# Sharing eleven semaphores among the transfers, and storing tile 58 in pieces of 48, 50 and 30 rows

## The chip, the cores and the metric

One core of one Trainium2 chip. The metric is device time in microseconds (us) of one execution. The span of a profile is about 1.8 us shorter than that time. All runs told here were in the fast state, and all gave the right result.

## The reference

```python
# x (16, 512, 1024), weight (1024, 768), bias (768), residual (16, 512, 768), all float32
def reference(x, weight, bias, residual):
    return (np.matmul(x, weight) + bias + residual).astype(np.float32)
```

That is 8192 rows: 64 tiles of 128 rows, with K = 1024 and N = 768. 61.9 MB are read and 25.2 MB written.

## The kernel before

The kernel records its operations in a list and then emits them with only the waits that they need. SyncE issues every transfer, in the order of a fixed list. An entry `('s', 3, 10, 11, 104)` stores tile 3 x 16 + 10 = 58, cut at row 104, so in two transfers of 104 and 24 rows. Each row of a tile is 3 KB.

```python
ORDER = [
 # ... loads of x, weight, bias and residual, and the stores of tiles 0 to 47
 ('s', 3, 0, 10), ('s', 3, 10, 11, 104), ('s', 3, 11, 13),          # tiles 48-57; 58; 59-60
 ('s', 3, 13, 14), ('s', 3, 14, 15), ('c', 3, 15, 0), ('c', 3, 15, 1)]   # 61; 62; 63 in two column parts

# in Program.emit, one semaphore for each transfer:
        for n, (eng, emit, _, dma) in enumerate(ops):
            e = self.engines[eng]
            for d in waits[n]:
                e.wait_ge(*mark[d])
            ins = emit(e)
            if dma:
                sem = self.tc.alloc_semaphore(f"landed_{n}")
                mark[n] = (sem, 16)
                ins.then_inc(sem, 16)
            # ... compute instructions count up the semaphore of their engine

# in pump(), a store with its cuts:
                edges = [0, *cut, P]
                for p0, p1 in zip(edges, edges[1:]):
                    dma(out_d[S, p0:p1, j0:j1, n0:n0 + nl],
                        R[p0:p1, t0 % RR:t0 % RR + j1 - j0, n0:n0 + nl], ...)   # cut
                    stores.append(len(prog.ops) - 1)

# at the end: all stores must have landed
        for sem, value in landed[:-OUTSIDE]:                 # OUTSIDE = 4
            nc.sync.wait_ge(sem, value)
    # ... and in a second critical section the last four, in reverse order
```

Of the kernel before, what the change touches and what calls it, by code (L numbers as in the profile page):

```python
# [31 lines left out]
 ('r', 0, 6, 16), ('x', 0, 14, 16), ('x', 1, 0, 6), ('r', 1, 0, 6), ('x', 1, 6, 16),  # L32
 ('r', 1, 6, 16), ('s', 0, 0, 16), ('x', 2, 0, 6), ('r', 2, 0, 6), ('x', 2, 6, 16),
 ('r', 2, 6, 16), ('s', 1, 0, 16), ('x', 3, 0, 6), ('r', 3, 0, 7), ('x', 3, 6, 16),
 ('r', 3, 7, 16), ('s', 2, 0, 16), ('s', 3, 0, 10), ('s', 3, 10, 11, 104), ('s', 3, 11, 13),
 ('s', 3, 13, 14), ('s', 3, 14, 15), ('c', 3, 15, 0), ('c', 3, 15, 1)]
OUTSIDE = 4
LAST = [(0, 512), (512, 256)]
# [2 lines left out]
class Program:  # L41
# [10 lines left out]
    def add(self, eng, emit, rd=(), wr=(), dma=False):  # L52
        n, ops = len(self.ops), self.ops
        deps = {self.writer[k] for k in (*rd, *wr) if k in self.writer and (eng != "pe" or ops[self.writer[k]][0] != eng)}
        for k in wr:
            deps.update(d for d in self.readers.get(k, ()) if ops[d][0] != eng or ops[d][3])
        for k in rd:
            self.readers.setdefault(k, set()).add(n)
        for k in wr:
            self.writer[k], self.readers[k] = n, set()  # L60
        self.ops.append((eng, emit, deps - {n}, dma))

    def emit(self, ends):

        ops, known = self.ops, {e: {} for e in self.engines}
        lane, count, snap, waits = [], {}, [], []
        for n, (eng, _, deps, dma) in enumerate(ops):
            mine = (n, 0) if dma else (eng, count.setdefault(eng, 0) + 1)
            if not dma:
                count[eng] += 1  # L70
            seen = known[eng]
            need = {}
            for d in deps:
                f, i = lane[d]
                if seen.get(f, -1) < i and i > need.get(f, (-1, 0))[0]:
                    need[f] = (i, d)
            need = {
                f: (i, d) for f, (i, d) in need.items()
                if not any(snap[d2].get(f, -1) >= i for g, (_, d2) in need.items() if g != f)
            }  # L80
            for f, (i, d) in need.items():
                for g, v in (*snap[d].items(), (f, i)):
                    if seen.get(g, -1) < v:
                        seen[g] = v
            waits.append([d for _, d in need.values()])
            lane.append(mine)
            own = dict(seen)
            own[mine[0]] = mine[1]
            snap.append(own)
        told = {d for w in waits for d in w}  # L90
        sems = {e: self.tc.alloc_semaphore(f"done_{e}") for e in self.engines if e != "sp"}
        total, mark = dict.fromkeys(self.engines, 0), {}
        for n, (eng, emit, _, dma) in enumerate(ops):
            e = self.engines[eng]
            for d in waits[n]:
                e.wait_ge(*mark[d])
            ins = emit(e)
            if dma:
                sem = self.tc.alloc_semaphore(f"landed_{n}")
                mark[n] = (sem, 16)  # L100
                ins.then_inc(sem, 16)
            elif n in told:
                total[eng] += 1
                mark[n] = (sems[eng], total[eng])
                ins.then_inc(sems[eng], 1)
        return [mark[n] for n in ends]
# [3 lines left out]
def kernel(  # L110
# [136 lines left out]
    def times(po, lhsT, rhs, first, final, rd, wr):  # L247
        def emit(e):
            return e.add_instruction(mybir.InstMatmult(  # L249
                name=nc.get_next_instruction_name(),  # L250
                ins=[e.lower_ap(rhs), e.lower_ap(lhsT, for_matmul_weights=True)], outs=[e.lower_ap(po)],
                start_tensor_calc=first, stop_tensor_calc=final,
                tile_size=(P, P), tile_position=(0, 0), ldweights=False,
            ))
        op("pe", emit, rd, wr)
# [144 lines left out]
```

## Time and profile before

| | before |
|---|---|
| time, median of 3 runs | 210.88 us (210.81 to 211.23) |
| span of the profile | 209.1 us |
| TensorE busy | 200.4 us, 96% |
| transfer queue, share of 16 engines | 97.7% |
| end of the last matmul | 204.1 us |

Two lines of the profile's page, kernel before: the busy share of the transfer engines in 40 slices of the span, in tenths, and what they moved.

```profile
DMA  6999999999989999999999999999999999998994
GB/s 222 424 429 436 432 414 471 391 449 411 495 377 486 389 410 418 442 447 407 428 450 450 411 423 479 404 423 412 424 482 423 421 415 472 451 432 366 441 360 162
```

Read them with the share of TensorE: two resources are nearly full at once. (The 16 engines that carry transfers are called transfer engines here. The records name no engine. The numbers 0 to 15 are labels: a store with 13 late counts is said to lie on engines 0 to 12, one with 12 on 0 to 11. Within a trace the rows bear such an order out: in the kernel before, twelve engines take ten rows of tile 58, one takes eight and three none. That an engine keeps its label in another execution or another kernel is an assumption.) TensorE ends at 204.1 us and the transfers run on behind it, so each can set the end, and only the last few microseconds tell which. The chain of waits, in order of time, shows the computing part of that end (columns: start, length, what):

```profile
198.89 5.21 PE psum_o L249 x32
204.11 0.02 issue
204.13 0.43 DVE ro L221
```

VectorE's last add is done at 204.56 us. The other 4.6 us of the span are stores landing and the closing barriers.

### The profile page before, as it was taken

The numbers are of one execution on the slowest core, as the hardware profiler recorded it, in microseconds if no ns is written. First come the engines' busy times: TensorE is split into PE (matmuls) and PEld (weight loads), VectorE is DVE, ScalarE is ACT, GpSimd is POOL, SyncE is SP. The second block draws the span as 40 slices with busy tenths as digits, with TensorE's granted clock in tenths as the row PEclk, the third lists the DMA queues.
The fourth block names the chain that finished last, engine by engine and source line by source line (L and its number), as shares of the span: only waits on it lengthen the run. The fifth ranks groups of instructions, "written<-read, shape, count | busy, mean of one in ns | idle before, by whom it ended". The sixth has DMA issues, their size and how long they took to land.

```text
span 209.1 us, 2471 instructions
## 1 busy us (share of the span) xinstructions
PE 200.4 (96%) x1273; PEld 80.9 (39%) x794; DVE 105.3 (50%) x141; ACT 66.1 (32%) x69; POOL 115.1 (55%) x71
## 2 busy tenths in 40 slices
PE   7899999999999999999999999999999999999990
PEld 2333433443443344344434433443443344344440
DVE  1458555445545544654455454645545544554451
ACT  2444513402640372310370093320091055330000
POOL 1100029759999805998039702999108950999000
PEclk9999999999999999999999999999999999999997
DMA  6999999999989999999999999999999999998994
GB/s 222 424 429 436 432 414 471 391 449 411 495 377 486 389 410 418 442 447 407 428 450 450 411 423 479 404 423 412 424 482 423 421 415 472 451 432 366 441 360 162
DMA packets 4924, 87.20 MB, mean 417 GB/s; under 512 B 557, under 2 KB 685, under 8 KB 1841
## 3 DMA queue, kind: packets, MB, share of 16 engines
q1 hardware_dynamic: 4913, 87.05, 97.7%
q8 instruction: 8, 0.13, 0.2%
q14 instruction: 3, 0.02, 0.0%
HBM read 61.88 MB, written 25.17 MB: 416 GB/s over the span
## 4 chain that ended last, share of the span: by engine, by line
PE 91%; DMA 4%; issue 1%; DVE 1%; SPq 0%; ACT 0%
PE psum_o L249 78%; PE pt L242 13%; DMA x_tile<-in_x_dram 4%; SPq L160 0%; DVE xt L218 0%; ACT xb L218 0%; DVE ro L221 0%; SPq L395 0%; SPq L363 0%
## 5 line engine op out<-in xcount | busy, mean ns | idle before, releaser
L249 PE MATMUL psum_o<-w_sb,xt 128*128 128x256 bf16 (+1 forms) x999 | 175.3, 324 | 1.8 <-DVE xt L218 0.5
L221 POOL TENSOR_TENSOR ro<-ro,bias_sb 128x768 f32<-128x768 f32 x50 | 88.8, 1811 | 46.8 <-DMA ro<-in_residual_dram 46.8
L218 ACT CAST xb<-x_tile 128x1024 bf16<-128x1024 f32 (+1 forms) x63 | 61.3, 1023 | 117.1 <-DMA x_tile<-in_x_dram 80.1
L260 PEld LDWEIGHTS <-xt 128*128 128x128 bf16 x520 | 50.9, 98 | 102.9 <-issue 101.0
L218 DVE COPY xt<-pt 128x1024 bf16<-128x1024 bf16 x64 | 44.1, 691 | 83.6 <-PE pt L242 83.6
L221 DVE TENSOR_TENSOR ro<-psum_o,ro 128x768 f32<-128x768 f32 (+2 forms) x51 | 47.6, 934 | 6.3 <-POOL ro L221 4.3
L242 PE MATMUL pt<-ident,xb 128*128 128x128 f32 x256 | 38.3, 273 | 0.5 <-DVE xb L218 0.3
L221 POOL TENSOR_TENSOR ro<-ro 128x768 f32<-128x768 f32 x14 | 24.9, 1813 | 25.0 <-DMA ro<-in_residual_dram 25.0
L242 PEld LDWEIGHTS pt<-ident,xb 128*128 128x128 f32 x256 | 29.7, 140 | 15.5 <-issue 12.3
L221 DVE TENSOR_TENSOR ro<-psum_o,bias_sb 128x768 f32<-128x768 f32 x14 | 13.2, 948 | 0.0
L304 PE MATMUL psum_o<-warm 128*128 128x512 bf16 x18 | 6.4, 514 | 1.4 <-DVE warm_a L224 1.4
L218 DVE CAST xb<-x_tile 128x512 bf16<-128x512 f32 (+1 forms) x4 | 1.9, 492 | 6.1 <-DMA x_tile<-in_x_dram 6.1
L218 ACT CAST w_sb<-ro 128x768 bf16<-128x768 f32 x4 | 3.3, 832 | 3.7 <-DMA ro<-in_weight_dram 3.7
L218 POOL CAST w_sb<-ro 128x768 bf16<-128x768 f32 x1 | 0.8, 824 | 5.9 <-DMA ro<-in_weight_dram 5.9
L304 PEld LDWEIGHTS psum_o<-warm 128*128 128x128 bf16 x18 | 2.2, 126 | 4.6 <-issue 2.9
L218 DVE CAST w_sb<-ro 128x768 bf16<-128x768 f32 x3 | 1.7, 557 | 2.0 <-DMA ro<-in_weight_dram 2.0
L218 ACT ACT_TABLE_LOAD x1 | 1.3, 1283 | 0.9 <-SPq L363 0.9
L321 DVE STREAM_SHUFFLE bias_sb<-bias_row 128x768 f32<-128x768 f32 x1 | 1.0, 1024 | 0.0
L224 DVE MEMSET warm<- 128x256 uint32 x1 | 0.3, 272 | 1.1 <-SPq L363 1.1
L224 DVE MEMSET bias_row<- 128x768 f32 x1 | 0.7, 698 | 0.2 <-issue 0.2
L224 POOL MEMSET ident<- 128x128 f32 x1 | 0.2, 204 | 0.5 <-SPq L363 0.5
L312 POOL TENSOR_SCALAR_AFFINE_SELECT ident<-ident 128x128 f32<-128x128 f32 x1 | 0.3, 293 | 0.2 <-POOL ident L224 0.2
(7 smaller groups left out, 0.7 us busy)
## 6 DMA issues: line engine op xcount, KB each, us to landing
out_dram<-ro SPq DMA_DIRECT2D x3, 6144.0 KB, 34.4
x_tile<-in_x_dram SPq DMA_DIRECT2D x3, 5120.0 KB, 24.5
ro<-in_residual_dram SPq DMA_DIRECT2D x3, 3840.0 KB, 32.1
x_tile<-in_x_dram SPq DMA_DIRECT2D x3, 3072.0 KB, 39.8
ro<-in_residual_dram SPq DMA_DIRECT2D x3, 2304.0 KB, 18.5
x_tile<-in_x_dram SPq DMA_DIRECT2D x4, 1024.0 KB, 10.9
x_tile<-in_x_dram SPq DMA_DIRECT2D x2, 2048.0 KB, 23.4
out_dram<-ro SPq DMA_DIRECT2D x1, 3840.0 KB, 13.1
```

Source lines behind the costliest of these rows:

```text
L218: op(eng, lambda e: (e.copy if eng == "act" else e.tensor_copy)(out=dst, in_=src), rd, wr)
L221: op(eng, lambda e: e.tensor_add(out=dst, in0=a, in1=b), rd, wr)
L224: op(eng, lambda e: e.memset(dst, v), [], [wr])
L242: op("pe", lambda e, q=q: e.transpose(out=pt[:, q, :], in_=words[:, ts(q, P)], identity=ident), [("XB", t % XB_N, 2 * q // n_q), "ident"], ...
L249: return e.add_instruction(mybir.InstMatmult(name=nc.get_next_instruction_name(), ins=[e.lower_ap(rhs), e.lower_ap(lhsT, for_matmul_weight ...
L260: op("pe", lambda g: g.ldweights(lhsT), rd)
L304: op("pe", lambda e: e.matmul(PO[i][:, 0:512], lhsT=warm[:, 0:P], rhs=warm, start=True, stop=True), ["warm"], [("PO", i)])
L312: op("pool", lambda e: e.affine_select(out=ident, in_=ident, compare_op=mybir.AluOpType.not_equal, fill=1.0, base=0, pattern=[[-1, P]], ch ...
L321: op("dve", lambda e: e.stream_shuffle(out=bias_sb, in_=bias_row, mask=[0] * QUAD), ["bias_row"], ["bias"])
```

## The change

The intent has two parts. A semaphore may serve a second transfer once SyncE has seen the first land, so eleven do for all, and fewer have to be cleared at the end. And the pieces of tile 58 are cut so that the transfer engines taken to be late get fewer of its rows.

```diff
- ('r', 3, 7, 16), ('s', 2, 0, 16), ('s', 3, 0, 10), ('s', 3, 10, 11, 104), ('s', 3, 11, 13),
+ ('r', 3, 7, 16), ('s', 2, 0, 16), ('s', 3, 0, 10), ('s', 3, 10, 11, 48, 98), ('s', 3, 11, 13),
@@ in emit
-        lane, count, snap, waits = [], {}, [], []
+        lane, count, snap, waits, slots, slot = [], {}, [], [], [], {}
@@
+            if dma:
+                free = [i for i, used in enumerate(slots) if seen.get(used[-1], -1) >= 0]
+                if not free:
+                    free = [len(slots)]
+                    slots.append([])
+                slot[n] = free[0], len(slots[free[0]]) + 1
+                slots[free[0]].append(n)
@@
+        landings = [self.tc.alloc_semaphore(f"landed_{i}") for i in range(len(slots))]
@@
-                sem = self.tc.alloc_semaphore(f"landed_{n}")
-                mark[n] = (sem, 16)
-                ins.then_inc(sem, 16)
+                i, k = slot[n]
+                mark[n] = (landings[i], 16 * k)
+                ins.then_inc(landings[i], 16)
```

The transfers go from 36 to 37 and the program's semaphores from 46 to 21: 36 and 11 for transfers, the other ten the same.

## The prediction

> **What bounds the kernel now.** I read the chain that ended last first, then the stretches after the last matmul, then the last stores, and at last the single records of stores and transfers in the same trace.
>
> ```profile
> ## 4 chain that ended last, share of the span: by engine, by line
> PE 91%; DMA 4%; issue 1%; DVE 1%; SPq 0%; ACT 0%
> ...
> q1 hardware_dynamic: 4913, 87.05, 97.7%
> q8 instruction: 8, 0.13, 0.2%
> ```
>
> TensorE carries the chain from about 10 us to 204.1 us of the 209.1 us span, and nothing in the change touches it. But the transfer queue is as full: 97.7% of 16 engines' time. So whatever a store leaves behind at the end cannot hide. Next, the stretches at the end (columns: stretch, its length, busy time and count of PE, PEld, DVE, ACT, POOL, then clock, DMA share, GB/s):
>
> ```profile
> 202.00:204.00 2.00, 2.00 (x14) 1.15 (x12) 1.16 (x2) 0.00 (x0) 0.00 (x0) 1.00 0.96 390
> 204.00:206.00 2.00, 0.09 (x1) 0.00 (x0) 0.44 (x2) 0.00 (x0) 0.00 (x0) 1.00 0.88 342
> 206.00:208.00 2.00, 0.00 (x0) 0.00 (x0) 0.00 (x0) 0.00 (x0) 0.00 (x0) 0.72 0.18 63
> 208.00:210.00 2.00, 0.00 (x0) 0.00 (x0) 0.00 (x0) 0.00 (x0) 0.00 (x0) 0.50 0.00 0
> ```
>
> After 204.1 us there is no computing, yet the transfer engines are 88% busy for two more us and 18% for a further two: a thinning queue, some engines done and others not. The last stores, by stretch (issue; size; us to landing):
>
> ```profile
> out_dram<-ro SPq DMA_DIRECT2D x1, 384.0 KB, 5.3
> ...
> out_dram<-ro SPq DMA_DIRECT2D x1, 384.0 KB, 4.2
> ...
> out_dram<-ro SPq DMA_DIRECT2D x1, 256.0 KB, 3.4
> out_dram<-ro SPq DMA_DIRECT2D x1, 128.0 KB, 3.2
> ```
>
> A store of 128 KB that takes 3.2 us stands behind others. Its 16 completion counts, one per engine, come from 206.37 to 207.74 us in the trace's records: fifteen have come by 207.23, and the last engine is another 0.51 later. SP then walks through barriers to 209.1. So **the end is set by the one slowest of the 16 transfer engines**.
>
> [...] the 104-row store has one early count and 13 later ones (k=13, 8 rows each), the 24-row store one and 12 (k=12, 2 rows each). Hence now: engines 0-11 take 10 rows of tile 58, engine 12 takes 8, engines 13-15 none. [...] the new code reuses a slot only after SP has seen its last transfer landed, so it needs no new wait and loses none. [...] 8 fetches of 16 KB (the q8 line), one each 24 us[...].
>
> **Who is the slowest engine.** I followed each engine through the packet records (a packet starts where the previous one of its engine ended). Up to 23 us the 16 engines finish within 0.54 us of each other. Each 16 KB fetch then throws a different single engine back by some 1.4 us (28 us: spread 1.95). At the end of the big ten-tile store ahead of tile 58 the engines stand at: never or little hit 198.85, 198.89, 198.97, 199.33, 199.62, 199.87, 200.31, 200.41; hit by fetches 1 to 8: 200.96, 200.83, 200.78, 200.65, 200.50, 200.54, 200.49, 200.93. The chains then tell numbers: the engine of fetch 2 runs 8 rows of 3 KB and goes on, so it is 12; those of fetches 3 and 4 run none (13-15), nor does the one at 199.33; those of fetches 1 and 8 run ten, so they lie in 0-11. The four that carried the 4-row bias load (k=4, engines 0-3) are all among the little hit. Fetches 1 to 4 on 11, 12, 13, 14 and then a wrap, so that fetch 8 falls on 10, fits all of this. **That 11 and 10 are the engines of fetches 1 and 8 is my inference**; the records do not say it.
>
> **The change part by part.**
> (a) *Split 48+50+30.* k = 16, 10, 15, with 3, 5 and 2 rows each: engines 0-9 keep 10 rows, 10-14 get 5, engine 15 gets 3. A row of 3 KB takes 0.118 us from start to start (trace). Now the engine of fetch 8 goes from 200.93 to 202.67: 10 x 0.118 = 1.18 plus 0.56, of which slow packets (267, 412 and 212 ns instead of 121) explain nearly all. From there it is never idle: 1.85 (768 KB store), 0.95, 0.95, 0.64, 0.35 us, its last packet ends at 207.41, and the count is visible 0.33 later: 207.74. After: engine 10 runs 5 rows, 200.93 + 0.59 = 201.52 (201.97 with as much slowness); engine 11: 200.96 + 0.59 = 201.55; 12: 201.42; 13: 201.37; 14: 201.24. New bound: the engines of fetches 5 to 7, still with 10 rows: 200.54 + 1.18 = 201.72, which is what they do now. Gain 202.67 - 201.72 = 0.95 us at most, 0.7 if engine 10 is slow again, 0.5 if slow packets hit another late engine. I take **0.75**.
> (b) *One more store to issue.* 0.35-0.45 us of SP's queue, at 191.4 us. The 24-row store now takes far longer to issue:
>
> ```profile
> 191.80 1.93 SPq L160 DMA_DIRECT2D out_dram<-ro  x1
> ```
>
> This and two other long issues (1.46 us at 95.7, 1.27 at 144.2) each stand beside an instruction fetch. Even with 2 us for the second and 0.5 for the third SP is free by 194.3; the next store is ready at 197.48, and no engine reaches tile 58 before 198.85. Cost **0**.
> (c) *Eleven semaphores.* Loads and stores keep their waits: the built programs show the same waits on PE, DVE, ACT and POOL, and on SP the same ones ahead of the transfers. After the last landing POOL clears the program's semaphores in one instruction of 287 ns, on the path to the end: 46 of them now (99 to 144), 21 after. If all 287 ns scale, 287 x 25/46 = 156 ns; allowing a fixed part I take **0.12 us**.
> (d) *Waits at the end.* SP checks early stores at 205.2, all long landed, then the last four in turn. One more early landing to check costs nothing while the last is still out.
>
> ```profile
> SPq L395 <- DMA out_dram<-ro: 1.6, 3, 0.6
> ```
>
> Sum: 0.75 + 0.12 = 0.87 us off 210.88, that is 210.0.
>
> **The rivals.** (1) *The numbering is wrong*, and the last engine is among 0-9: it keeps its 10 rows, in three pieces, and only the clear is saved: 210.75. For it: the inference above. Against: 104+24 spared 12-15 already, and a second cut that spares 10 and 11 as well makes sense only if those are the late ones. (2) *Fetch positions differ from run to run*, so that sparing fixed engines wins only sometimes: 210.0 to 210.9, with more scatter. For it: one trace shows one execution. Against: four times within 210.81-211.23. (3) *The issue of the third piece blocks* until the big store is done (201.4) and delays the 768 KB store by up to 4 us: the queue runs dry and the end moves by one to two us, 212. Against: the blocked issues ended beside fetches, not landings. (4) *The tail is hidden anyway*, because the last store's own latency binds: its fastest count came 1.2 us after its issue ended (205.17 to 206.37), so the floor is 206.4, 1.3 below the present end. It does not bind at the gain that I claim. Sharing itself could only hurt through an added wait, and the built program has none.
>
> **Range and chances.** With the numbering right (some 75%) 209.8 to 210.4; with it wrong 210.6 to 210.8; run to run 0.2. So 210.05 with 209.6 to 210.75. Two per cent is 4.2 us, and the whole tail after the last matmul is 5: faster by over 2% has 0.01, slower (rival 3 at its worst) 0.01.
>
> **What would show it.** Tile 58's pieces show 16, 10 and 15 late counts. The last store's counts spread over less than 1 us instead of 1.37 and end near 206.8-207.0; time from its issue to landing falls from 3.2 to about 2.4 us. The clear takes 130 to 170 ns. TensorE still ends at 204.1. The prediction is wrong if the last count stays at 207.7, if the clear stays at 287 ns, if the 768 KB store is issued after 197.5, or if TensorE's end moves.

k is the number of a transfer's late counts. That 48, 50 and 30 rows would give 16, 10 and 15 of them could not be read from the trace of the kernel before; the trace of the changed kernel shows it, with one early count for each of the two smaller k, at 193.53 and 194.77 us.

## The result, and the profile after

| | before, same rounds | after |
|---|---|---|
| median | 210.68 us (210.48 to 211.23, 6 runs) | 210.45 us (210.26 to 210.75, 6 runs) |
| ratio | | 0.9986, 95% interval 0.9971 to 1.0001 |

All outputs are right. A ratio here is the mean time of one kernel's runs over the mean of the other's runs of the same rounds, so it is not quite the ratio of the medians quoted. The verdict is "same". The gain is 0.23 us by medians and about 0.3 us by means, and its interval reaches zero. The profiled run took 210.75 us and is the slowest of the six, so its trace is not the typical one.

The page of the changed kernel: the chain's header and the queues.

```profile
PE 91%; DMA 4%; issue 1%; ACT 1%; DVE 1%; SPq 0%
...
q1 hardware_dynamic: 4929, 87.05, 97.9%
q8 instruction: 8, 0.13, 0.2%
```

Nothing moved: the same chain, the same bytes in sixteen more packets, the same eight instruction fetches. Next the end in two-microsecond stretches, changed kernel (columns as in the prediction):

```profile
202.00:204.00 2.00, 2.00 (x14) 1.17 (x12) 1.16 (x2) 0.00 (x0) 0.00 (x0) 1.00 0.97 396
204.00:206.00 2.00, 0.40 (x4) 0.11 (x2) 0.75 (x2) 0.00 (x0) 0.00 (x0) 1.00 0.95 371
206.00:208.00 2.00, 0.00 (x0) 0.00 (x0) 0.00 (x0) 0.00 (x0) 0.00 (x0) 0.99 0.24 87
208.00:210.00 2.00, 0.00 (x0) 0.00 (x0) 0.00 (x0) 0.00 (x0) 0.00 (x0) 0.50 0.00 0
```

TensorE works 0.31 us more after 204 (0.40 against 0.09), and the transfer engines are busier in 204 to 206 and again in 206 to 208. The tail did not get thinner. The chain of waits at its end, changed kernel:

```profile
199.20 5.21 PE psum_o L257 x32
204.41 0.02 issue
204.44 0.43 DVE ro L229
```

The last 32 matmuls take 5.21 us as before, but begin 0.31 later. The last stores, changed kernel:

```profile
out_dram<-ro SPq DMA_DIRECT2D x1, 384.0 KB, 3.9
out_dram<-ro SPq DMA_DIRECT2D x1, 256.0 KB, 3.0
out_dram<-ro SPq DMA_DIRECT2D x1, 128.0 KB, 2.8
```

The last store takes 2.8 us instead of 3.2, not the 2.4 predicted, and it was issued later because TensorE ended later. Its sixteen counts come from 206.55 to 207.72 us, where the kernel before had 206.37 to 207.74. The last count is where it was. The issue of tile 58's three pieces, and SyncE's checks at the end:

```profile
191.71 2.89 SPq L168 DMA_DIRECT2D out_dram<-ro  x3
```

```profile
SPq L403 <- DMA out_dram<-ro: 1.4, 3, 0.6
```

SyncE is free again at 194.60 us and the next store is issued at 197.78, as VectorE frees it: the additional piece blocks nothing. In this pair of traces the span goes from 209.14 to 208.96 us, and 0.16 of these 0.18 us lie behind the last count: 1.24 us pass from there to the end instead of 1.40. The clearing of the semaphores, in the records of the trace, takes 157 ns instead of 287.

### The profile page after: what moved, and what is told of

It reads as the page before. It is cut to its first block, busy times and chain, and to the rows that moved or that the text cites. A ratio compares the mean times of both kernels' runs of the same rounds, so it can differ in the third digit from the quotient of the medians.

```text
span 209.0 us, 2473 instructions
## 1 busy us (share of the span) xinstructions
PE 201.0 (96%) x1273; PEld 80.9 (39%) x794; DVE 105.3 (50%) x141; ACT 66.1 (32%) x69; POOL 115.2 (55%) x71
## 4 chain that ended last, share of the span: by engine, by line
PE 91%; DMA 4%; issue 1%; ACT 1%; DVE 1%; SPq 0%
PE psum_o L257 78%; PE pt L250 13%; DMA x_tile<-in_x_dram 4%; ACT xb L226 1%; SPq L168 0%; DVE xt L226 0%; DVE ro L229 0%; SPq L403 0%; SPq L371 0%
## 5 line engine op out<-in xcount | busy, mean ns | idle before, releaser
L312 PE MATMUL psum_o<-warm 128*128 128x512 bf16 x18 | 6.9, 547 | 1.4 <-DVE warm_a L232 1.4
```

The source lines that it names most:

```text
L312: op("pe", lambda e: e.matmul(PO[i][:, 0:512], lhsT=warm[:, 0:P], rhs=warm, start=True, stop=True), ["warm"], [("PO", i)])
```

## How the experiments are read

A difference of 0.1% is within the noise of the times, so each kernel's trace is used too. From the records of each profiled run I took the last count of the ten-tile store ahead of tile 58 (A), the last count of tile 58 (B), the last count of all (C), how many of the 3 KB packets after 198 us took over 200 ns instead of 121, the clear, and the time from C to the end of the span. "Rows by engine" is how tile 58 falls on the 16 engines by the late counts of its pieces. Each trace is one execution, and not always a typical one: E7, E8, E10 and E11 were profiled in the fastest of their runs (E7 at 210.09 us, the next at 210.38), the changed kernel and the kernel before, again, in the slowest.

```
kernel                cuts    rows by engine        A       B     B-A     C     C-B  slow clear end-C
before                104     10x12, 8, 0x3      201.44  203.00  1.57  207.74  4.74   11   287  1.40
before, again         104     the same           201.33  203.05  1.72  207.78  4.72   12   288  1.40
E1 semaphores only    104     the same           201.71  202.51  0.79  207.38  4.87    5   157  1.24
changed               48,98   10x10, 5x5, 3      201.88  202.99  1.11  207.72  4.73    9   157  1.24
changed, again (E9)   48,98   the same           201.55  202.37  0.82  207.23  4.86   12   157  1.24
E2 split only         48,98   the same           201.43  202.67  1.24  207.53  4.86    7   290  1.41
E4 seven engines      49,113  12x7, 5x8, 4       201.97  202.91  0.94  207.60  4.70   18   157  1.24
E11 four engines      68      21x4, 4x11, 0      201.33  203.40  2.06  208.13  4.73    5   157  1.24
E3 uncut              none    8x16               201.53  202.44  0.91  207.09  4.66    0   157  1.24
E10 uncut again       none    8x16               201.28  202.19  0.91  206.94  4.75    0   157  1.24
E5 uncut, own sems    none    8x16               201.75  202.67  0.92  207.31  4.64    0   287  1.40
E8 uncut, spare sems  none    8x16               201.44  202.36  0.92  206.99  4.63    0   287  1.40
E6 two halves         64      8x16               201.48  202.41  0.93  207.04  4.63    7   157  1.24
E7 even three         48,112  8x16               201.38  202.38  1.00  207.02  4.64    4   157  1.24
```

Two things hold in all fourteen rows. C is B plus 4.6 to 4.9 us, wherever VectorE's last add ended (204.54 to 204.95): behind tile 58 the slowest engine has a fixed load and no gap, so **the slowest transfer engine sets the end**. And A wanders by 0.69 us from one execution to the next without any cut having been reached.

My theory after the result: the clear is worth its 0.16 us, and the split takes rows from engines that are late only in part. Rivals: the split works and chance hid it in one trace; sharing semaphores costs something elsewhere; the late engines have other fixed numbers, 7 to 14.

## The experiments

In each diff the line removed is that of the changed kernel unless said otherwise. The kernel before ran with medians of 210.72, 210.71 and 210.86 us. Kernels are compared only within the same rounds.

**E1, the semaphores alone.** Tile 58 cut as before.

```diff
-('s', 3, 10, 11, 48, 98)
+('s', 3, 10, 11, 104)
```

> The eleven shared semaphores alone, tile 58 stored in 104 and 24 rows as before. My theory, in which the clear at the end scales with the number of semaphores (287 ns for 46, 157 ns for 21): 0.13 us less than the kernel before, ratio 0.9994; the counts of the last store spread over 1.3 to 1.4 us as before. Rival (the whole of the 0.29 us gained comes from the semaphores, the split does nothing): 0.29 us less, ratio 0.9986. Rival (sharing adds a wait somewhere): above 1.

Measured: 210.40 us, ratio 0.9982 (0.9969 to 0.9994). So the semaphores alone do all that the whole change does; adding the split to them brings nothing that these times can see. The time is where the first rival put it (0.9986), lower than my 0.9994, and the counts of the last store spread over 0.93 us, not 1.3 to 1.4: two misses. The span behind the last count is 1.24 us, as in the changed kernel.

**E2, the split alone.** The kernel before with the new cuts.

```diff
-('s', 3, 10, 11, 104)        # kernel before
+('s', 3, 10, 11, 48, 98)
```

> The three pieces of tile 58 alone, a semaphore for each transfer as before. My theory (the end is the slowest transfer engine; the rows taken off engines 10 and 11 shorten it, but slow packets on an engine below 10 give most back): 0.15 to 0.2 us less than before, ratio 0.9991 to 0.9993, clear at 287 ns, counts of the last store spread over 1.1 to 1.2 us. Rival (semaphores do it all): ratio 1.0. First forecast on record: 0.75 us less, ratio 0.9964.

Measured: 210.56 us, ratio 0.9993 (0.9981 to 1.0006). The split by itself is worth 0.15 us with an interval of -0.13 to 0.40: not told from zero, and 0.75 us lies well outside. The clear is back at 290 ns.

**E3, tile 58 not cut at all.**

```diff
-('s', 3, 10, 11, 48, 98)
+('s', 3, 10, 11)
```

> Eleven semaphores and tile 58 stored in one transfer of 128 rows (16 engines, 8 rows each). [...] there are no 3 KB packets above 200 ns in tile 58, and the last engine ends it at its own start plus 0.95 us: some 0.2 us sooner than in the changed kernel, so the time is 0.1 to 0.3 us below it (ratio to before 0.9975 to 0.998). Rival (what counts is rows on the late engines, slow packets come anyhow): the late engines carry 8 rows instead of 5 and the time is 0.2 to 0.4 us above the changed kernel, at or above the kernel before (ratio 0.9995 to 1.001).

Measured: 210.11 us, ratio 0.9973 (0.9961 to 0.9986), the fastest so far. Every engine takes eight rows, and none of the 3 KB packets is slow. Both cuts have the longer time; against the changed kernel the difference is not clear of the noise. How the uncut store is issued (start, length):

```profile
191.39 0.33 SPq L168 DMA_DIRECT2D out_dram<-ro  x1
```

It is issued in 0.33 us, where three pieces took 2.89. That difference costs nothing, as SyncE then waits for the next tile until after 197 us.

**E4, other engines spared.** 49 + 64 + 15 rows came with k = 7, 16 and 15: engines 0 to 6 take 12 rows, 7 to 14 five, 15 four. If the eight late engines were 7 to 14, this would be the best cut.

```diff
-('s', 3, 10, 11, 48, 98)
+('s', 3, 10, 11, 49, 113)
```

> Eleven semaphores and tile 58 in pieces of 49, 64 and 15 rows (7, 16 and 15 engines): engines 0 to 6 carry 12 rows, 7 to 14 carry 5, engine 15 carries 4. If the eight engines set back by instruction fetches are 7 to 14, this relieves all of them: the last engine ends tile 58 some 0.4 to 0.6 us sooner than in the changed kernel, ratio to before 0.996 to 0.9975, spread of the last store's counts 0.6 to 0.9 us. Rival (the numbering is wrong and late engines lie among 0 to 6): they carry 12 rows instead of 10, the end moves 0.2 us later than in the changed kernel, ratio 0.9995 or more. Rival (slow packets follow the pieces, whatever their size): the same as the changed kernel, 0.9985.

Measured: 210.62 us, ratio 0.9994 (0.998 to 1.0008). The trace refutes that numbering: two engines that come early (198.98 and 199.01 us) run only five rows, so lie in 7 to 14, and the engines of fetches 5 and 6, late at 200.40 and 200.63, run twelve, so lie in 0 to 6.

**E5, uncut with a semaphore for each transfer** (the kernel before without its cut).

```diff
-('s', 3, 10, 11, 104)        # kernel before
+('s', 3, 10, 11)
```

> The kernel before with tile 58 in one transfer of 128 rows, a semaphore for each transfer (45 to clear). My theory now (pieces cost slow packets on the late engines, the uncut store none; sharing saves only the clear): 0.4 to 0.5 us below the kernel before, ratio 0.9977 to 0.9981, clear at some 285 ns, no 3 KB packet above 200 ns. Rival (sharing saves more than the clear, and the uncut store gains little): ratio 0.9990 or more.

Measured: 210.52 us, ratio 0.9992 (0.9979 to 1.0006). By time this is level with the kernel before, as the rival had it; my 0.9977 to 0.9981 missed. So the times do not show that the uncut store alone gains anything. By the trace B-A is 0.92 us as in E3, and the clear takes 287 ns as before. Its A, 201.75, was among the late ones.

**E8, uncut, shared semaphores, and 24 more that nothing uses.** If the number of semaphores is what costs, the clear must be back; if sharing itself matters, it stays short.

```diff
+        for i in range(24):
+            self.tc.alloc_semaphore(f"spare_{i}")
```

> The uncut kernel with eleven shared semaphores, and 24 more allocated that nobody uses, so that again 45 are cleared. If only the number cleared matters, it equals the uncut kernel with a semaphore for each transfer within 0.1 us (clear 280 to 290 ns). If sharing itself saves time, it lies 0.1 to 0.2 us below that kernel, at the 0.9973 of the uncut kernel before.

Measured: 210.35 us, ratio 0.9987 (0.9975 to 1.0), against 0.9973 for E3. The clear, of 45 semaphores now, takes 287 ns again, and 1.40 us pass from the last count to the end. So for the clear it is the number allocated that counts, not the sharing. The times of E8 and E5, with 45 semaphores each, lie 0.17 us apart and are not told apart.

**E6, two even halves.** Eight rows on every engine, but in two transfers.

```diff
-('s', 3, 10, 11, 48, 98)
+('s', 3, 10, 11, 64)
```

> Eleven semaphores, tile 58 in two pieces of 64 rows: 16 engines with 4 and 4 rows, so 8 rows on each engine exactly as in the uncut store, [...] at least four 3 KB packets above 200 ns, the last engine ends tile 58 more than 1.1 us after its own start instead of 0.95, and the time is 0.15 to 0.5 us above the uncut kernel (ratio to before 0.998 to 0.9995). Rival (only the rows of each engine count): the same as the uncut kernel, 0.9973.

Measured: 210.20 us, ratio 0.9981 (0.9968 to 0.9994). My expectation that slow packets alone would lift B-A above 1.1 us missed: seven slow packets are there, up to 562 ns, but all on engines that are early, and B-A stays 0.93. The time lies in the range that I gave (0.998 to 0.9995) and is not told apart from the rival's 0.9973.

**E7, three even pieces** of 48, 64 and 16 rows.

```diff
-('s', 3, 10, 11, 48, 98)
+('s', 3, 10, 11, 48, 112)
```

> Eleven semaphores, tile 58 in 48, 64 and 16 rows: as many pieces as in the changed kernel, but 3, 4 and 1 rows on each of the 16 engines, 8 in all. If the pieces themselves cost (slow packets), it is like the changed kernel, 0.998 to 0.999. If the cost of the changed kernel is the ten rows on the late engines among 0 to 9, this one has eight there and lies 0.2 us below the changed kernel, near 0.9975.

Measured: 210.48 us, ratio 0.9989 (0.9977 to 1.0002). B-A is 1.00, with four slow packets, so in this trace three even pieces cost next to nothing. But it is the trace of the fastest of the five runs, and their median lies where I had put it if the pieces themselves cost. Whether the number of pieces or the rows on the late engines matters more is not shown.

**E9, E10, E12, three kernels again** on another chip: the changed one, the uncut one and the one before, without edits.

> The changed kernel once more, unaltered. Time again 0.2 to 0.4 us below before (ratio 0.998 to 0.999). In the trace: if the order in which instruction fetches fall on the transfer engines is fixed, the engine of fetch 8 is again one of 10 to 14 and the late engines among 0 to 9 are those of the same fetches as in the first trace of this kernel. If it turns from execution to execution (my theory now), the same eight engines are late (10 to 14 and three below 10, never 15), but by other fetches.

> The uncut kernel with eleven semaphores once more, beside the changed kernel on one chip. My theory (8 rows and no slow packets on the late engines beat 10 rows with them): from the last VectorE add to the last count 2.2 to 2.6 us, where the changed kernel has 2.6 to 2.9; time 0.1 to 0.3 us below the changed kernel. Rival (the cut makes no difference that can be seen): within 0.1 us of it.

> The kernel before against itself: what the noise of such a comparison is. Ratio 1.000, and by the intervals seen so far within 0.001 of it. In the trace, fetches 1 and 8 need not fall on engines with ten rows again; engines 10 to 14 are late, 15 is not; from the last VectorE add to the last count 2.6 to 3.2 us.

Measured: changed 210.32 us, ratio 0.998 (0.9961 to 1.0); uncut 210.16, ratio 0.9969 (0.9951 to 0.9987); before 210.70, ratio 0.9994 (0.9976 to 1.0011). The last is the noise: a kernel against itself. E10's six runs lie within 210.00 and 210.27, E9's within 210.06 and 211.04. Uncut over changed is 210.15 over 210.41 by means, 0.9987, but one run of 211.04 makes half of that.

In E9's trace my theory missed and the first alternative came true: fetch 8 is again on an engine with five rows, so one of 10 to 14, and the late engines with ten rows are again those of fetches 3 to 5. These two executions do not show the order turning; the two of the kernel before do. From VectorE's last add to the last count it has 2.39 us where I expected 2.6 to 2.9, no longer than E10's 2.36. In E12 the expectation held: fetch 8 is on an engine without rows of tile 58, and the tail is 3.16 us. The end of the uncut kernel, E10, first its stretches and then its last two stores:

```profile
204.00:206.00 2.00, 0.13 (x2) 0.00 (x0) 0.48 (x2) 0.00 (x0) 0.00 (x0) 1.00 0.90 347
206.00:208.00 2.00, 0.00 (x0) 0.00 (x0) 0.00 (x0) 0.00 (x0) 0.00 (x0) 1.00 0.10 36
```

```profile
out_dram<-ro SPq DMA_DIRECT2D x1, 256.0 KB, 2.5
out_dram<-ro SPq DMA_DIRECT2D x1, 128.0 KB, 2.3
```

The queue is as busy up to 206 us, but only 10% of it runs after that, where the kernel before had 18% and the changed one 24%, and the last store lands after 2.3 us. These shares vary between executions: 10 to 18% in the four uncut traces, 16 and 18% in those of the kernel before, 20 and 24% in those of the changed one.

**E11, an overdose.** 68 + 60 rows came with k = 4 and 15: engines 0 to 3 take 21 rows, 4 to 14 four, 15 none. If the slowest engine sets the end, B-A must grow even though these four are seldom late.

```diff
-('s', 3, 10, 11, 48, 98)
+('s', 3, 10, 11, 68)
```

> Eleven semaphores, tile 58 in 68 and 60 rows (4 and 15 engines): 21 rows on engines 0 to 3, 4 on 4 to 14, none on 15. If engines 0 to 3 are not among those that fetches of 16 KB throw back, they end it near 199.2 + 2.5 = 201.7 us and the late ones near 201.4 + 0.5 = 201.9, so the tail is no longer than the uncut kernel's (2.2 to 2.6 us). If a late engine lies among them it ends at 203.4 or later, and the tail is over 3.5 us, the time 0.8 us above the uncut kernel.

Measured: 211.59 us, ratio 1.0036 (1.0017 to 1.0055), the only kernel slower than the one before. One of the four engines had been set back by about 1 us near 60 us, by a smaller fetch of 8 KB; it stood at 200.19, spent 2.87 us on its 21 rows, and was the last. I had thought of the 16 KB fetches alone. The tail is 3.44 us, and the time is 1.43 us above the uncut kernel in the same rounds, not 0.8. Stretch and last stores of this kernel:

```profile
206.00:208.00 2.00, 0.00 (x0) 0.00 (x0) 0.00 (x0) 0.00 (x0) 0.00 (x0) 1.00 0.28 101
```

```profile
out_dram<-ro SPq DMA_DIRECT2D x1, 256.0 KB, 3.6
out_dram<-ro SPq DMA_DIRECT2D x1, 128.0 KB, 3.4
```

28% after 206 us and 3.4 us to land: the opposite of the uncut kernel. B-A went to 2.06 and C with it.

## Why the prediction was right or wrong

**Right: the range.** 210.45 us lies in 209.6 to 210.75. Of the 0.40 us to the point at 210.05, 0.20 is the kernel before, which ran at 210.68 in the same rounds and not at 210.88. The rest is the gain: 0.87 us predicted, 0.2 to 0.3 measured. That the time lies in the range is in part luck: the range held both the gain of the split (209.8 to 210.4) and its absence (210.6 to 210.8), and 210.45 lies between the two.

**Right: the bound.** That the end is set by the slowest of the 16 transfer engines is what C-B of 4.6 to 4.9 us in all traces says, and E11 shows it by dose.

**Right: (b), (c) and (d).** The piece more cost nothing at issue, so rival 3 falls. The clear fell from 287 to 157 ns, and all in all 0.16 us are saved behind the last count where 0.12 was put down. In time, semaphores alone gave ratios of 0.9982 (E1); by trace 0.16 us is all I can point to, and if there is more, it is not shown.

**Wrong: (a), the term of 0.75 us.** It was sized as the way from 202.67 to a new bound, "the engines of fetches 5 to 7, still with 10 rows", at 201.72. That bound is the step that failed: the changed kernel's last engine was done with tile 58 at 202.64. The measured worth of the split is 0 to 0.15 us, with an interval that ends at 0.40 (E2). Three things took its place.

1. *The order of the fetches turns from one execution to the next.* This was rival 2. It need not turn each time (E9), but it can. In the traces of this pair a fetch of 16 KB took 0.89 to 1.10 us and the packet behind it 0.37 to 0.55 us more than others of its size, 1.3 to 1.6 us together for its engine; a fetch of 8 KB took 0.31 to 0.32 and cost 0.27 to 0.66 behind it, 0.6 to 1.0 together. In the first trace of the kernel before, engine 12 is that of fetch 2, by its eight rows, and engines 13 to 15, which take none, hold fetches 3 and 4 and the one engine not hit. In the second trace of the same kernel engines 13 to 15 hold fetch 8 and fetch 2 or 7. What is steady, by these labels, is the set: wherever row counts tell, engines 10 to 14 are late and three more late ones lie below 10. Engine 15 is not late (it is done with the ten-tile store at 199.26 to 199.54 in the five traces that single it out; in three more, one of 13 to 15 is, at 199.19 to 199.43).

   A clue that I had overlooked puts this in order. On its engine, the packet after a fetch takes longer than others of its size. For fetches 1 to 7 this excess is 466, 481, 550, 549, 494, 497 and 505 ns in the changed kernel, and the same within 2 ns in E9. In the kernel before it is 506, 467, 467, 481, 548, 549 and 494: the same series, entered two places earlier. That each value belongs to one engine, so that the eight engines come round in one order, is my estimate from these series: every row count that I could follow fits it, but no record names an engine. By it fetches 1 and 8 of the first trace did lie on engines 10 and 11. If it holds, the numbering that the prediction inferred was right for that trace, rival 1 falls, and the cut did aim at the engine that had been last.
2. *So the new bound is not at 201.72.* The three late engines below 10 keep ten rows, whichever fetches fell on them. In the changed kernel's trace these were fetches 3 to 5, and engines with ten rows stood at 200.61, 200.69, 200.89 and 201.01. The last of them ran ten rows at 0.118 us, 1.18, plus 0.45 for packets of 222, 336 and 222 ns, and was done at 202.64. So of the 0.92 us above 201.72, 0.47 is the later start and 0.45 the slow packets. In the kernel before the last went from 200.93 to 202.67, with packets of 267, 412 and 222 ns (the prediction has 212 for the third). The same end, by this estimate on a different engine, and with nearly as much slowness.
3. *Slow packets come with the cut.* All ten cut traces have 4 to 18 of them, the four uncut ones none, on any engine. With even pieces (E6, E7) those seen fell on early engines and cost at most 0.09 us of B-A; with uneven ones they fell on late engines in several traces. The prediction had allowed for "slow again" only as a lower gain.

That C did not move at all in the first pair is in part chance: the ten-tile store ended 0.44 us later in the changed kernel's trace (201.88 against 201.44), so B-A did fall there, from 1.57 to 1.11. But B-A of the three traces of the new split, 0.82 to 1.24, overlaps that of the three traces of the old cut, 0.79 to 1.72, and in time E1 and the changed kernel are level.

**What else the profile was to show.** The pieces had their 16, 10 and 15 late counts. The other transfers followed in the traces had 16 for 128, 64, 48 and 16 rows, 13 for 104, 12 for 24 and 4 for the 4 rows of the bias; in E4 49 and 15 rows had 7 and 15, in E11 68 and 60 had 4 and 15. No rule beyond these cases is shown. TensorE ended at 204.41 us and not at 204.1, and the 768 KB store was issued at 197.78 and not by 197.5. Both were named as signs that the prediction is wrong, and they are not: over the traces VectorE's last add moves by 0.4 us and C does not follow. The spread of the last counts, 1.17 us, and their end at 207.72 are the signs that did tell.

**Left open.** Why packets of a cut store are slow. The records show no packet over 200 ns in the four uncut traces and 4 to 18 in every cut one; the longest took 833 ns. They tell neither what a packet reads nor what slows it; the order of rows that the expectations of E3 and E6 gave as a possible reason was a guess, and is cut from them. Nor is it shown why engine 15 gets no fetch, or why TensorE ended 0.31 us later in the changed kernel's trace. And an advantage of the uncut store over the changed kernel of 0.1% is smaller than what the intervals resolve; its ratio to the kernel before excludes 1.

**A version that beats the kernel before**, and is at least level with the changed one, is therefore the changed kernel without any cut (E3, E10): shared semaphores, tile 58 in one transfer, 0.9973 and 0.9969 of the kernel before, and with fewer transfers than either.

## What to carry to other kernels

Where the transfer queue is full to the end (97.7% here, and C-B 4.6 to 4.9 us in every trace), ask which of the 16 engines is the last and how many rows the last stores give it, not how many bytes move in all; a store whose rows fall evenly on all 16 asks for no guess about which are late. Do not aim a cut at engines from one trace: take a second trace of the same kernel first, and ask which late engine becomes the last once the one you aim at is relieved. Semaphores that are allocated but not needed cost some 5 ns each at the end, an estimate from the clear: 287 to 290 ns for 45 or 46 of them, 157 ns for 21. For time differences of a tenth of a per cent look at counts in the trace too, but in several traces: one execution can be the slowest or the fastest of its kind.
